# Chunk output matrices before most input matrices, and input matrices that stay on the chip

## Chip, cores, metric

The kernel runs on one core of a Trainium2 chip. The metric is the device time of one execution in microseconds; a comparison goes by the median of several executions.

## The reference, cut to what matters

A two-layer backbone over 1024 latent tokens of 1024 channels and 256 context tokens. The first layer holds 48 groups of a bidirectional linear recurrence (S5) beside an FNet part; the second is pooling and short convolutions. The change lies in the recurrence of the first layer:

```python
def s5_direction(u, lam_re, lam_im, log_step, b_re, b_im, c_re, c_im):
    lam = lax.complex(lam_re, lam_im)
    step = jnp.exp(log_step)[:, None]
    lam_bar = jnp.exp(lam * step)
    b_bar = ((lam_bar - 1.0) / lam)[..., None] * lax.complex(b_re, b_im)
    bu = lax.complex(jnp.einsum('btgh,gph->btgp', u, b_bar.real),
                     jnp.einsum('btgh,gph->btgp', u, b_bar.imag))
    a = jnp.broadcast_to(lam_bar, bu.shape)
    _, s = lax.associative_scan(_linear_recurrence, (a, bu), axis=1)
    return (jnp.einsum('btgp,ghp->btgh', s.real, c_re) - jnp.einsum('btgp,ghp->btgh', s.imag, c_im))
```

It is run over context and latents together, once forward and once backward; u is the first 768 columns of the layer's input projection.

## The kernel before

Channels lie on the 128 partitions. Products are made in three matmuls of split operands (a high part and a low remainder), so each weight tile is first split by `w_split`: ScalarE (ACT) writes the high part, VectorE (DVE) or GpSimd (POOL) subtracts for the low part. TensorE (PE) executes in the order in which the program emits; so does every other engine, and every DMA queue (SP's, POOL's). The program's order is written out by hand: `proj` calls a hook after each of its 8 contraction steps k, and the hook emits other work there.

The recurrence is taken in chunks of 8 steps. For each of 6 blocks b and two halves hf, that is 4 groups at a time:
- a `bl_task` builds an input matrix: five DVE operations write `bl` (with `blp` as scratch), then eight PE transposes and two ACT copies make `bltw`, which POOL's queue stores in DRAM (`bltd`);
- a `cl_task` builds an output matrix: five DVE operations write `cl` (two buffers), two DMAs on SP's queue store it (`cld`), and 32 small matmuls `pz`, ACT copies and two short DVE operations (`dg`, `z`) make the direct term `z`, stored in `zd`;
- `bl_mm(i)` multiplies input matrix i (`blt`, loaded from `bltd`) with the chunked inputs (`ub`, loaded from `ud`) in 32 matmuls, and ACT copies the result into `va` (i under 6) or `vb`.

The order: prelude; then for m = 0 to 5 the projection of 128 columns, 32 per block, to `ut` and its context part `uc` to `utc`, both stored in `ud` by POOL's queue (m = 0 and 1 were multiplied in the prelude). From m = 1 on `fill` is called by the hooks and after each context part: it emits the DVE part of the next task (all 12 bl, then all 12 cl) and, two tasks behind it, that task's PE part. Loads of `blt` and `ub` start in m = 4. Then `fx(0, hook0)` is a projection whose hook emits chunks 0 to 5 and the remaining cl tasks; chunks 6 to 11 follow with `tree(0, l)`, a five-level combination of the context part on `va` (DVE), then `tree(1)` on `vb`, and 121 double scan steps on DVE beside `fx(1)` and eight more projections on PE. Then the outputs are formed (y stage), and the rest of both layers follows.

Two shared sets of buffers matter. `slot` gives one of 8 buffers of 4 KB a partition (tag "slot"); a new tile takes the one given back longest ago, and its first writer waits for the last reader of the old tile. It holds `ut`, `utc`, `bltw`, `blt`, `ub`, `fx`, `zt`. In PSUM there are 4 banks with the tag "m" (`uc`, `pt`, `pz`, a part of the chunk products `vps`) and 4 with "acc" (projections, the rest of `vps`). `raw`, the unsplit weights, has 4 buffers, filled from SP's queue.

Of the kernel before, what the change touches and what calls it, by code (L numbers as in the profile page):

```python
# [194 lines left out]
class Builder:  # L195
# [218 lines left out]
    def s5_prelim(self, tp, s5s, raw):  # L414
# [57 lines left out]
        self.bbs = self.gp.tile([P, NG, 16], F32, name="bbs")  # L472

        def inputs():

            nc.vector.memset(self.bb[:, :, NG], 0.0)
# [12 lines left out]
        self.pwb = self.gp.tile([P, 3, NG, 8], F32, name="pwb")  # L489
        self.pwc = self.kp.tile([P, 3, 9, NG], F32, name="pwc")  # L490
# [15 lines left out]
    def bl_task(self, b, hf):  # L506
# [15 lines left out]
        def pe():  # L522
            blt = self.slot("bltw").rearrange("p (r g n) -> p r g n", r=2, g=4)
            for ri in range(2):
                pt = self.ps("m", "pt")
                for g in range(4):
                    nc.tensor.transpose(pt[:, g * P:g * P + P], bl[:, ri, g].rearrange("p h s -> p (h s)"),  # L527
                                        self.c("ident"))
                self.act(blt[:, ri].rearrange("p g n -> p (g n)"), pt)
            nc.gpsimd.dma_start(self.bltd[b][:, :, 4 * hf:4 * hf + 4], blt)  # L530
        return dve, pe

    def cl_task(self, b, hf):
# [6 lines left out]
        def dve():  # L540
# [165 lines left out]
    def build(self):  # L706
        nc, tc, A = self.nc, self.tc, self.A
        with ExitStack() as es:
# [13 lines left out]
            self.bltd = [self.drp.tile([P, 2, 8, P], F32, name=f"bltd{b}") for b in range(6)]  # L722
# [25 lines left out]
    def layer0(self, es):  # L748
# [5 lines left out]
        self.kp = kx.enter_context(tc.tile_pool(name="kp", bufs=1, side="right"))  # L754
        pwx = ExitStack()
# [183 lines left out]
        tables(0)  # L939
        inputs = inputs()  # L940
        for _ in range(4):
            next(inputs)


        ax = ExitStack()
# [12 lines left out]
        self.sq = nc.sync  # L958
# [19 lines left out]
        blq = []  # L978

        def bl_load(i):  # L980
            b, hf = divmod(i, 2)
            blt = self.slot("blt").rearrange("p (r g n) -> p r g n", r=2, g=4)
            nc.sync.dma_start(blt, self.bltd[b][:, :, 4 * hf:4 * hf + 4])
            ub = self.slot("ub")[:, 0:768].rearrange("p (g j) -> p g j", g=4)
            nc.sync.dma_start(ub, self.ud[b][4 * hf:4 * hf + 4].rearrange("g h s j -> (h s) g j"))
            blq.append((blt, ub))

        for m in range(6):
            if m == 5:
                bl_load(2)  # L990
# [5 lines left out]
            else:  # L996
                self.w_split(names[m + 1])
                self.proj((hi, lo), hr, 8, lambda p, c0, c1: self.act(ut[:, c0:c1], p),
                          hook=(lambda k: fill() if k in ((2, 4, 6, 7) if m == 2 else (0, 2, 4, 6)) else None))
            if m == 1:  # L1000
                tables(1)
                sx.close()
                self.gt = ax.enter_context(tc.tile_pool(name="gt", bufs=1))
                self.kt = kx.enter_context(tc.tile_pool(name="kt", bufs=1, side="right"))
# [21 lines left out]
        ax.close()  # L1026
# [5 lines left out]
        v = [vx.enter_context(tc.tile_pool(name="va", bufs=1)).tile([P, NSTEP, 2, NH], F32, name="va")]  # L1032

        def bl_mm(i):
            blt, ub = blq.pop(0)
# [13 lines left out]
            if i + 3 < 12:  # L1049
                bl_load(i + 3)  # L1050

        blk = list(range(12))
        self.sq = nc.gpsimd

        def fx(ct, hook):
            x = self.slot("fx")
# [3 lines left out]
            self.proj(hl, hr, 8, lambda p, c0, c1: self.act(x[:, c0:c1], p), hook=hook)  # L1060
            return lambda: nc.gpsimd.dma_start(xd[:, ct], x)
# [7 lines left out]
        while pend:  # L1069
            fill()  # L1070
        flush()
        kx.close()
        v.append(vx.enter_context(tc.tile_pool(name="vb", bufs=1, reuse_waits="tile")).tile([P, NSTEP, 2, NH], F32, name="vb"))

        scx = ExitStack()
        scp = scx.enter_context(tc.tile_pool(name="scp", bufs=1, reuse_waits="tile"))
        cf = [self.acf] + [scp.tile([P, 2, 2, NG], F32, name=f"acf{l}") for l in range(1, 5)]

        def square(l):
            r, i = cf[l - 1][:, 0, 0], cf[l - 1][:, 1, 0]  # L1080
            o = cf[l]
            self.mul(o[:, 0, 0], r, r)
            self.mul(o[:, 0, 1], i, i)
            self.stt(o[:, 1, 0], r, 2.0, i, ALU.mult, ALU.mult)
            self.sub(o[:, 0, 0], o[:, 0, 0], o[:, 0, 1])
            self.stt(o[:, 1, 1], r, -2.0, i, ALU.mult, ALU.mult)
# [735 lines left out]
```

## Time and profile before

| | us |
|---|---|
| median of 3 executions | 923.29 (922.24 to 925.9) |
| the profiled execution's own time | 923.49 |
| its span, first to last instruction | 921.7 |
| PE busy in the span | 866.0 (94%) |
| DVE busy | 671.9 (73%) |
| ACT busy | 344.1 (37%) |

The profile is of one execution. Its trace gives start and duration of each instruction, the idle time ahead of it and what ended that (`<-`), and for DMAs when they were issued and when they landed. Matmuls are pipelined, so the duration of one is longer than its share of the time; the distance of starts is what counts. Line 218 is the helper of DVE's additions, subtractions and products, 243 that of ACT's copies, 373 the split matmuls of all projections.

### The profile page before, as it was taken

Reading aid. Unit: us, or ns where it says so; the run is one execution under the profiler, and the core shown is the slowest. Engines: PE = TensorE matmul, PEld = TensorE weight load, DVE = VectorE, ACT = ScalarE, POOL = GpSimd, SP = SyncE. Lnnn points to the kernel's source line nnn. Section 1 sums busy time; section 2 is a strip of 40 time slices with the busy share of each in tenths; the row PEclk is TensorE's granted clock in tenths of the full one; section 3 lists DMA queues with packets and bytes.
Section 4 is the critical chain, followed back from the end, with each engine's and each line's share of the span. In section 5 each row is a group of like instructions: output and inputs, shape, how many; then the busy total and the mean of one; then the engine's idle time right before and its main releaser. Section 6 shows DMA issues by size and latency. Waiting matters only on the chain.

```text
span 921.7 us, 14134 instructions
## 1 busy us (share of the span) xinstructions
PE 866.0 (94%) x5312; PEld 707.6 (77%) x5312; DVE 671.9 (73%) x1736; ACT 344.1 (37%) x593; POOL 94.1 (10%) x91
## 2 busy tenths in 40 slices
PE   9998997989999959899999999999999999989996
PEld 4666785768777738787888999877778778768995
DVE  7787996868999996556367376788885766775354
ACT  5547331465113129644342144542222233453111
POOL 0002330212122203200034001000000000000000
PEclk9999998999999988899999999999999999999998
DMA  9743779891555557931264212121111121261022
GB/s 353 293 137 115 241 215 281 237 368 62 172 217 207 194 172 211 307 127 54 69 250 135 102 41 69 46 58 46 46 47 46 46 65 51 69 228 45 1 92 92
DMA packets 62212, 129.16 MB, mean 140 GB/s; under 512 B 5760, under 2 KB 32560, under 8 KB 62016
## 3 DMA queue, kind: packets, MB, share of 16 engines
q1 hardware_dynamic: 55280, 104.45, 34.2%
q0 software_dynamic: 6864, 23.81, 8.3%
q8 instruction: 42, 0.69, 0.3%
q14 instruction: 26, 0.21, 0.1%
HBM read 100.03 MB, written 28.21 MB: 139 GB/s over the span
## 4 chain that ended last, share of the span: by engine, by line
PE 58%; DVE 26%; ACT 7%; DMA 5%; issue 2%; SPq 1%; ACTq 0%; DVEq 0%; POOL 0%
PE acc L373 32%; PE acc L1743 14%; DVE va L218 11%; DVE vb L218 2%; DVE wlo L218 2%; PE yps L1205 2%; PE acc L883 2%; ACT vb L243 1%; DMA mt<-zd 1%; DVE hh L218 1%; ACT whi L243 1%; DVE tl L218 1%; PE pt L527 1%; DVE xt L218 1%; DMA blt<-bltd 1%
## 5 line engine op out<-in xcount | busy, mean ns | idle before, releaser
L373 PE MATMUL acc<-hh,whi 128*128 128x512 f32 (+1 forms) x352 | 112.1, 385 | 2.5 <-ACT whi L243 2.5
L373 PE MATMUL acc<-hl,whi 128*128 128x512 f32 (+1 forms) x352 | 108.8, 376 | 0.0
L373 PE MATMUL acc<-hh,wlo 128*128 128x512 f32 (+1 forms) x352 | 108.6, 375 | 0.1
L373 PEld LDWEIGHTS acc<-hh,whi 128*128 128x128 f32 x352 | 62.9, 189 | 17.6 <-issue 5.0
L373 PEld LDWEIGHTS acc<-hh,wlo 128*128 128x128 f32 x352 | 65.4, 189 | 13.4 <-DVE wlo L218 0.5
L373 PEld LDWEIGHTS acc<-hl,whi 128*128 128x128 f32 x352 | 65.4, 189 | 13.1
L243 ACT ACTIVATE whi<-hh 128x512 fp32r<-128x512 f32 (+4 forms) x44 | 27.7, 632 | 114.6 <-DVE hh L218 86.0
L218 DVE TENSOR_TENSOR wlo<-raw,whi 128x512 fp32r<-128x512 f32 (+3 forms) x57 | 48.5, 855 | 28.7 <-ACT whi L243 28.2
L243 ACT ACTIVATE whi<-raw 128x512 fp32r<-128x512 f32 (+3 forms) x65 | 51.8, 801 | 42.7 <-PE acc L1743 20.8
L1743 PE MATMUL acc<-th,whi 128*128 128x512 f32 x160 | 63.1, 394 | 0.0
L1743 PE MATMUL acc<-tl,whi 128*128 128x512 f32 x160 | 62.4, 390 | 0.3 <-DVE tl L218 0.3
L218 DVE TENSOR_TENSOR va<-va 128x48 f32<-128x48 f32 (+1 forms) x258 | 62.3, 243 | 0.4
L1743 PE MATMUL acc<-th,wlo 128*128 128x512 f32 x160 | 62.3, 390 | 0.0
L239 DVE SCALAR_TENSOR_TENSOR xl<-acc,adac,xl 128x256 f32<-128x256 f32 (+1 forms) x48 | 27.3, 569 | 41.5 <-PE acc L373 41.1
L218 DVE TENSOR_TENSOR wlo<-hh,whi 128x512 fp32r<-128x512 f32 (+4 forms) x44 | 30.4, 690 | 31.7 <-ACT whi L243 30.9
L1743 PE MATMUL acc<-hh,whi 128*128 128x512 f32 x120 | 48.4, 403 | 5.2 <-DVE y L218 2.5
L1743 PE MATMUL acc<-hh,wlo 128*128 128x512 f32 x120 | 47.5, 396 | 0.3 <-DVE wlo L218 0.3
L1743 PE MATMUL acc<-hl,whi 128*128 128x512 f32 x120 | 47.5, 396 | 0.0
L373 PE MATMUL acc<-hh,wh 128*128 128x256 f32 (+1 forms) x144 | 46.2, 321 | 0.0
L373 PE MATMUL acc<-th,hh 128*128 128x256 f32 (+1 forms) x144 | 46.2, 321 | 0.0
L373 PE MATMUL acc<-hh,wl 128*128 128x256 f32 (+1 forms) x144 | 46.1, 320 | 0.0
L373 PE MATMUL acc<-hl,wh 128*128 128x256 f32 (+1 forms) x144 | 45.9, 318 | 0.0
(295 smaller groups left out, 2125.5 us busy)
## 6 DMA issues: line engine op xcount, KB each, us to landing
raw<-in_ada SPq DMA_DIRECT2D x44, 512.0 KB, 5.7
raw<-in_win SPq DMA_DIRECT2D x38, 512.0 KB, 3.6
raw<-in_wout SPq DMA_DIRECT2D x16, 512.0 KB, 3.7
bltd<-bltw POOLq DMA_DIRECT2D x12, 512.0 KB, 4.9
blt<-bltd SPq DMA_DIRECT2D x12, 512.0 KB, 8.5
cl<-cld POOLq DMA_DIRECT2D x12, 512.0 KB, 6.4
cld<-cl SPq DMA_DIRECT2D x18, 256.0 KB, 5.1
ub<-ud SPq DMA_DIRECT2D x12, 384.0 KB, 7.6
```

The lines of the kernel that those rows point to most:

```text
L218: (eng or self.nc.vector).tensor_tensor(out, a, b, op=op)
L239: self.nc.vector.scalar_tensor_tensor(out, a, s, b, op0=op0, op1=op1)
L243: self.nc.scalar.activation(out, a, func, **kw)
L373: self.nc.tensor.matmul(p, a[:, w], b[:, c0:c1], start=(j == 0 and i == 0), stop=(last and i == 2))
L527: nc.tensor.transpose(pt[:, g * P:g * P + P], bl[:, ri, g].rearrange("p h s -> p (h s)"), self.c("ident"))
L883: nc.tensor.matmul(acc[m][h], a[:, w], b[:, 512 * h:512 * h + 512], start=(k == 0 and i == 0), stop=(k == 7 and i == 2))
L1205: nc.tensor.matmul(ps[:, o], sy[:, ri, g], cl[:, ri, g], start=False, stop=(ri == 1))
L1743: nc.tensor.matmul(ps, x[:, sl], y, start=bool(new and k == 0 and i == 0), stop=(k == 3 and i == 2), skip_group_check=True)
```

## The change

Input matrices are no longer stored in DRAM and loaded: ACT copies the transposes into a slot (`blt`) from which `bl_mm` reads. `bl` becomes a slot, `blp` a PSUM tile of tag "m", `bbs` a slot. The order of tasks becomes: bl 0 to 2, all 12 cl, bl 3 and 4 in m = 1 to 5 (17 calls of `fill`); then `chunk(i)` emits, for i over 2, the transposes of matrix i, the product, and the DVE part of matrix i + 2, so that bl 5 to 11 are built between the chunks. Chunks 0 to 9 now lie in the hooks of `fx(0)`: two after k = 0, two after k = 1, one after each other k; `square` and `tree(0)` follow chunk 5 in the hook of k = 3 and take three slots; chunks 10 and 11 follow, with the split of weight 8 and six scan steps of `va` between them. `ub` is loaded two chunks ahead, from after the loop on. `cld` and `zd` are stored by POOL's queue. `tables(0)` (ACT's six `pwb` copies) moves from the end of the prelude to m = 0, behind the split of weight 2. Slots for `fx` and `zt` are taken when they are first written. `va` and `vb` are opened together.

```diff
@@ bl_task
-        bl = self.gt.tile([P, 2, 4, 16, 8], F32, tag="bl", name="bl", bufs=2)
+        bl = self.slot("bl").rearrange("p (r g h s) -> p r g h s", r=2, g=4, h=16)
-            p = self.gt.tile([P, 4, 16, 8], F32, tag="blp", name="blp", bufs=1)
+            p = self.ps("m", "blp").rearrange("p (g h s) -> p g h s", g=4, h=16)
-            blt = self.slot("bltw").rearrange("p (r g n) -> p r g n", r=2, g=4)
+            blt = self.slot("blt").rearrange("p (r g n) -> p r g n", r=2, g=4)
...
-            nc.gpsimd.dma_start(self.bltd[b][:, :, 4 * hf:4 * hf + 4], blt)
+            self.blts.append(blt)
@@ cl_task
-                self.sq.dma_start(self.cld[b][r, :, 4 * hf:4 * hf + 4], cl[r, :, :, o:o + 128])
+                nc.gpsimd.dma_start(self.cld[b][r, :, 4 * hf:4 * hf + 4], cl[r, :, :, o:o + 128])
@@ layer0
-        tables(0)
         inputs = inputs()
-        for _ in range(4):
+        for _ in range(2):
             next(inputs)
...
-        todo = []
-        for b in range(6):
-            todo += [(self.bl_task, b, 0), (self.bl_task, b, 1)]
-        for b in range(6):
-            todo += [(self.cl_task, b, 0), (self.cl_task, b, 1)]
+        bls = [(self.bl_task, b, hf) for b in range(6) for hf in range(2)]
+        todo = bls[:3] + [(self.cl_task, b, hf) for b in range(6) for hf in range(2)] + bls[3:5]
+        bls = bls[5:]
...
-                self.sq.dma_start(self.zd[b].rearrange("a p e -> p a e"), z)
+                nc.gpsimd.dma_start(self.zd[b].rearrange("a p e -> p a e"), z)
...
-            if len(pend) == 2 or not todo:
-                if pend:
-                    pend.pop(0)()
+            if len(pend) == 2:
+                pend.pop(0)()
...
-            if m == 4:
-                bl_load(0)
-                bl_load(1)
...
             if m == 0:
                 self.w_split(names[2])
+                tables(0)
                 for _ in inputs:
                     pass
-            else:
+            elif m < 3:
                 fill()
...
+        while todo:
+            fill()
+        flush()
+        kqx.close()
...
+        ub_load(0)
+        ub_load(1)
 
         def bl_mm(i):
-            blt, ub = blq.pop(0)
+            blt, ub = self.blts.pop(0), ubq.pop(0)
...
-            if i + 3 < 12:
-                bl_load(i + 3)
+            ub_load(i + 2)
+
+        def chunk(i):
+
+            if i > 2:
+                pend.pop(0)()
+            bl_mm(i)
+            if i > 2 and bls:
+                f, b, hf = bls.pop(0)
+                t = f(b, hf)
+                t[0]()
+                pend.append(t[1])
...
+        def square():
+
+            t = self.slot("acf")[:, 0:16 * NG].rearrange("p (l k r g) -> p l k r g", l=4, k=2, r=2)
...
+        def tree(c):
+
+            tr = [self.slot("tr") for k in range(2)]
+            for l in range(5):
...
         def hook0(k):
-            if k not in (2, 5):
-                bl_mm(blk.pop(0))
-                fill()
+            for i in {0: (0, 1), 1: (2, 3)}.get(k, (k + 2,)):
+                chunk(i)
+            if k == 3:
+                square()
+                tree(0)
...
-        while blk:
-            bl_mm(blk.pop(0))
-            if len(blk) == 0:
-                self.w_split(names[8], nc.gpsimd)
-            if len(blk) < 5:
-                tree(0, 4 - len(blk))
+        chunk(10)
+        self.w_split(names[8], nc.gpsimd)
         for i in range(NC_, NC_ + SKEW):
             step((0, i))()
-        for l in range(5):
-            tree(1, l)
+        chunk(11)
+        kx.close()
+        tree(1)
```

## Rows read from the trace of the kernel before

**Rows 1.** Stretches: us, busy of PE, PEld, DVE, ACT, POOL, PEclk, DMA share, GB/s.

```profile
81.85:162.30 80.45, 74.05 (x553) 58.57 (x554) 69.94 (x112) 29.21 (x64) 20.47 (x27) 0.96 0.82 247
162.30:214.70 52.40, 47.72 (x650) 39.72 (x648) 37.59 (x105) 31.98 (x65) 9.79 (x13) 1.00 0.88 278
330.60:341.70 11.10, 2.21 (x34) 1.09 (x28) 11.10 (x83) 1.20 (x3) 0.71 (x1) 0.78 0.35 94
```

**Rows 2.** Chain of waits, 60 to 230 us: start, us, what.

```profile
193.22 8.78 DMA blt<-bltd
```

**Rows 3.** Timeline around the start of m=2: start, us, engine, line, operation [idle <-releaser].

```profile
74.01 5.60 ACT L243 ACTIVATE pwb<-pw 64x384 f32<-64x384 f32 x6
80.74 1.06 ACT L243 ACTIVATE whi<-raw 128x1024 fp32r<-128x1024 f32 x1
81.85 0.73 PE L373 MATMUL acc<-hh,whi 128*128 128x512 f32 x2 [2.47 <-ACT whi L243]
```

**Rows 4.** DVE's timeline in m=2 to 5, and a group from the groups by line.

```profile
94.32 0.69 DVE L218 TENSOR_TENSOR blp<-bbs,pwb 128x512 f32<-128x512 f32 x1
...
97.46 0.69 DVE L218 TENSOR_TENSOR blp<-bbs,pwb 128x512 f32<-128x512 f32 x1
...
140.93 0.23 DVE L239 SCALAR_TENSOR_TENSOR dg<-cst,vec,pz 128x16 f32<-128x16 f32 x1
...
144.62 1.22 DVE L218 TENSOR_TENSOR wlo<-raw,whi 128x1024 fp32r<-128x1024 f32 x1
...
L218 DVE TENSOR_TENSOR hl<-acc,hl 128x512 f32<-128x512 f32 x20 | 13.7, 683 | 0.0
```

**Rows 5.** Chain of waits, PE's pieces in m=2 to 5.

```profile
107.27 0.87 PE pt L527 x8
108.15 2.80 PE acc L373 x12
116.90 2.87 PE uc L373 x24
133.11 0.64 PE pz L566 x32
```

**Rows 6.** Instructions by tile: bltw; then landings of tiles ut, ub and cl.

```profile
L243 ACT ACTIVATE bltw<-pt x24: 592/598/603, 90.4 to 130.4; 128x512 f32<-128x512 f32 x24
L530 POOL DMA_DIRECT2D bltd<-bltw x12: 667/676/1156, 91.8 to 131.3; - x12
...
DMA to landing us min/median/max: 4.0/5.0/6.2
...
DMA to landing us min/median/max: 4.9/7.6/13.6
...
DMA to landing us min/median/max: 3.4/6.5/8.9
```

**Rows 7.** PE's timeline, first matmuls of two neighbouring chunks.

```profile
209.86 0.32 PE L1042 MATMUL vps<-ub,blt 128*64 128x160 f32 x1
...
212.27 0.32 PE L1042 MATMUL vps<-ub,blt 128*64 128x160 f32 x1
```

**Rows 8.** DVE's timeline: squares, tree(0), first scan step.

```profile
194.87 0.32 DVE L218 TENSOR_TENSOR acf<-acf 128x48 f32<-128x48 f32 x2
...
198.84 1.82 DVE L218 TENSOR_TENSOR tr<-va,acf 128x768 f32<-128x768 f32 x2 [1.11 <-ACT va L243]
200.59 1.94 DVE L218 TENSOR_TENSOR va<-va,tr 128x768 f32<-128x768 f32 x2
...
207.66 0.26 DVE L218 TENSOR_TENSOR va<-va,acf 128x96 f32<-128x96 f32 x1
```

**Rows 9.** Stretch after a wait of PE; columns as in rows 1.

```profile
157.67:162.73 5.06, 5.03 (x41) 3.62 (x42) 3.00 (x7) 1.54 (x6) 0.00 (x0) 0.50 1.02 286
```

**Rows 10.** Timelines of DVE and POOL at tree(1).

```profile
217.55 4.14 DVE L218 TENSOR_TENSOR vb<-vb,tr 128x768 f32<-128x768 f32 x2
...
216.72 3.17 POOL L218 TENSOR_TENSOR wlo<-raw,whi 128x1024 fp32r<-128x1024 f32 x1 [16.15 <-ACT whi L243]
```

More of the change, by code (lines that the diff above doesn't have):

```diff
@@ L471, in s5_prelim @@
         self.bb = self.kp.tile([P, 2, NG + 1, 16], F32, name="bb")
[L472 removed]
         def inputs():
+            self.bbs = self.slot("bbs")[:, 0:NG * 16].rearrange("p (g h) -> p g h", g=NG)
             nc.vector.memset(self.bb[:, :, NG], 0.0)
@@ L486, in inputs @@
                 yield
-        self.pwb = self.gp.tile([P, 3, NG, 8], F32, name="pwb")
-        self.pwc = self.kp.tile([P, 3, 9, NG], F32, name="pwc")
+        self.pwb = self.kp.tile([P, 3, NG, 8], F32, name="pwb")
+        self.pwc = self.kq.tile([P, 3, 9, NG], F32, name="pwc")
         self.acf = self.pwp.tile([P, 2, 2, NG], F32, name="acf")
@@ L998, in layer0 @@
                 self.proj((hi, lo), hr, 8, lambda p, c0, c1: self.act(ut[:, c0:c1], p),
-                          hook=(lambda k: fill() if k in ((2, 4, 6, 7) if m == 2 else (0, 2, 4, 6)) else None))
+                          hook=lambda k: fill() if k in ((2, 4, 6) if m == 2 else (0, 2, 4, 6)) else None)
             if m == 1:
@@ L1048, in bl_mm @@
                     self.act(dst, src)
-            if i + 3 < 12:
-                bl_load(i + 3)
-        blk = list(range(12))
-        self.sq = nc.gpsimd
+            ub_load(i + 2)
[8 more added lines that the diff above has]
+                pend.append(t[1])
+        cf = [self.acf]
+        def square():
+            t = self.slot("acf")[:, 0:16 * NG].rearrange("p (l k r g) -> p l k r g", l=4, k=2, r=2)
+            cf.extend(t[:, l] for l in range(4))
+            for l in range(1, 5):
+                r, i = cf[l - 1][:, 0, 0], cf[l - 1][:, 1, 0]
+                o = cf[l]
+                self.mul(o[:, 0, 0], r, r)
+                self.mul(o[:, 0, 1], i, i)
+                self.stt(o[:, 1, 0], r, 2.0, i, ALU.mult, ALU.mult)
+                self.sub(o[:, 0, 0], o[:, 0, 0], o[:, 0, 1])
+                self.stt(o[:, 1, 1], r, -2.0, i, ALU.mult, ALU.mult)
+                nc.vector.tensor_copy(o[:, 0, 1], o[:, 0, 0])
+        def tree(c):
+            tr = [self.slot("tr") for k in range(2)]
+            for l in range(5):
+                n = NC_ >> (l + 1)
+                d = 1 << l
+                a, b = (v[c][:, k * d - 1:NC_:2 * d] for k in (1, 2))
+                gs = slice(NH * c, NH * c + NH)
+                tm = [t[:, 0:2 * NH * n].rearrange("p (n r g) -> p n r g", n=n, r=2) for t in tr]
+                for k in range(2):
+                    self.mul(tm[k], a, cf[l][:, k, :, gs].unsqueeze(1).to_broadcast([P, n, 2, NH]))
+                self.add(b, b, tm[0])
+                self.add(b, b, tm[1][:, :, ::-1])
         def fx(ct, hook):
-            x = self.slot("fx")
             hl = self.w_take(names[6 + ct])
@@ L1059, in fx, with evac @@
                 self.w_split(names[7])
-            self.proj(hl, hr, 8, lambda p, c0, c1: self.act(x[:, c0:c1], p), hook=hook)
-            return lambda: nc.gpsimd.dma_start(xd[:, ct], x)
-        def hook0(k):
-            if k not in (2, 5):
-                bl_mm(blk.pop(0))
-                fill()
-        fx(0, hook0)()
[L1069 to L1086, printed above, removed]
-            nc.vector.tensor_copy(o[:, 0, 1], o[:, 0, 0])
-        def tree(c, l):
-            n = NC_ >> (l + 1)
-            d = 1 << l
-            a, b = (v[c][:, k * d - 1:NC_:2 * d] for k in (1, 2))
-            gs = slice(NH * c, NH * c + NH)
-            tm = [scp.tile([P, NC_ // 2, 2, NH], F32, tag=f"tr{k}", name="tr", bufs=1)[:, 0:n] for k in range(2)]
-            for k in range(2):
-                self.mul(tm[k], a, cf[l][:, k, :, gs].unsqueeze(1).to_broadcast([P, n, 2, NH]))
-            self.add(b, b, tm[0])
-            self.add(b, b, tm[1][:, :, ::-1])
+            x = []
+            def evac(p, c0, c1):
+                if not x:
+                    x.append(self.slot("fx"))
+                self.act(x[0][:, c0:c1], p)
+            self.proj(hl, hr, 8, evac, hook=hook)
+            return lambda: nc.gpsimd.dma_start(xd[:, ct], x[0])
+        def hook0(k):
+            for i in {0: (0, 1), 1: (2, 3)}.get(k, (k + 2,)):
[3 more added lines that the diff above has]
+                tree(0)
+        fx(0, hook0)()
         def step(*ci):
@@ L1117, in step @@
             return f
-        for l in range(1, 5):
-            square(l)
-        while blk:
-            bl_mm(blk.pop(0))
-            if len(blk) == 0:
-                self.w_split(names[8], nc.gpsimd)
-            if len(blk) < 5:
-                tree(0, 4 - len(blk))
+        chunk(10)
+        self.w_split(names[8], nc.gpsimd)
         for i in range(NC_, NC_ + SKEW):
             step((0, i))()
-        for l in range(5):
-            tree(1, l)
+        chunk(11)
+        kx.close()
+        tree(1)
         n = NSTEP - 1
@@ L1136, in layer0 @@
         store = fx(1, lambda k: self.bg(2 if k % 4 else 1))
-        zt = [self.slot(f"zt{k}") for k in range(KD)]
+        zt = []
         gates = [(0, ch) for ch in range(8, 12)] + [(1, ch) for ch in range(12)]
```

37 lines of the change are left out of this document (18 added, 19 removed).

## The prediction

> **What bounds the kernel now.** I read the table of stretches first. It shows TensorE (PE) busy nearly everywhere, so a gain must come from its gaps and from places where VectorE (DVE) sets the end. Two stretches belong to the change: 81.85 to 162.3 us (input projections m=2 to 5, with 12 input-matrix and 6 output-matrix tasks between them; PE idles 6.4 us) and 162.3 to 214.7 us (the fx projection with the 12 chunk inputs; 4.7 us). Then DVE runs tree(1) and the scan steps without a break, and PE has run out of work at 330.6 to 341.7, where it is busy 2.2 of 11.1 us while DVE is busy all of it [rows 1]. So what follows the last chunk hangs on DVE, and an earlier last chunk moves the end one for one. I therefore follow three times: when m=2 starts, t0 = the end of projection m=5 (162.3), and the end of the last chunk (214.7). The chain of waits names the DMA round trip of the input matrices in the second stretch: reading one back took 8.8 us [rows 2].
>
> **The head.** Today ScalarE (ACT) makes the six `pwb` copies (5.60 us) ahead of `ut` and of the split of weight 2, and PE waits 2.47 us for that split [rows 3]. The change moves `tables(0)` behind the split. The split then ends at about 76.2, its low half on DVE at 77.6, and PE starts m=2 at 79.4. The copies now precede `utc`, the second `ut` and `pwc`, so the split of weight 3 still ends near 88.6: DVE waits about 3 us for it after the first input-matrix task, and the second task ends at 92.9. PE meets its transposes at 89.8 and stalls 3.1 us; a few waits of under 1 us bring this to 4.4.
>
> **m=2 to 5.** A bl task takes DVE 3.13 us, a cl task with its `dg` 3.69, a low half 1.14 (from 94.32 to 97.46, from 140.93 to 144.62, and its row of 1.22 less the overlap with the next) [rows 4]. `blp` in PSUM I take at no cost: a same-sized DVE add with a PSUM operand took 683 ns, as the SBUF ones do [rows 4]; the bounds are 0 and some 0.1 us for each of 3 operations in 12 tasks, hidden where DVE waits. On PE one k of a projection takes 1.40, a context part 2.87, a set of transposes 0.87, a `pz` 0.7 (0.64 in its row, and a little to start) [rows 5]. From 79.4 to t0: 32 k at 1.40 (44.9) + 3 context parts (8.6) + 3 transposes (2.6) + 12 pz (8.4) = 64.5, + 4.4 idle = 68.9, so 148.3. DVE needs in the same time bl0 to bl2, twelve cl and four low halves, and reaches cl11 at 144, just ahead of PE's last hook. They are balanced, and the cover is thin.
>
> The `cld` stores go from SP to POOL's queue. Two cl buffers mean that cl task i+2 writes only when store i has landed. POOL issued the 512 KB stores in 0.68 us each; `cld` stores landed 3.4 to 8.9 us after issue, median 6.5 [rows 6]. With two issues of 0.75 and a landing in light traffic I take 5.5 us from the end of the task to the landing; two tasks then need 2.67 + 5.5 = 8.2 us, against PE's 8.5 (17.05 for each m with 4 tasks). So little is lost; 0 to 6 us, I take 1.2, nearer the free end because 12 stores and all read-backs of the input matrices leave. POOL's in-order queue also puts `ud` stores behind `cld` stores, which nobody awaits before m=5. t0 = 149.5, which is 12.8 earlier.
>
> The 12 stores and 12 loads of input matrices that go free 12 issues of POOL and 12 of SP (0.68 us and more each); no engine waits for these issues, so that is worth nothing but quieter DMA. The `zd` stores move to POOL as well; their buffers come round only every fourth task, so I put them at nothing, covered by two tasks of 3.69.
>
> A rule bears on this move. In this trace POOL's issue took 0.68 us while DVE computed almost without pause [rows 4, 6]. The Trainium skill (SBUF — State Buffer, section SBUF: two separate sides) says that GpSimd writes the descriptors of such DMAs and is locked out while DVE runs an operation in a two-port mode. If these DVE operations were of that kind, each of a task's two issues would wait for up to one of them, and the sum would be that of the slower rival below; the trace disagrees for these operations.
>
> **After t0.** PE's own work is a context part 2.9 + fx 11.2 + 12 chunks at 2.41 [rows 7] (28.9) + 9 transposes that moved here (7.8) = 50.8, against 52.4 measured with all its idle time [rows 1]. So nothing is gained here, and three things are added.
>
> First, the loads of `ub`. Until now they start during m=4. In the change `ub_load(0)` and `(1)` stand behind the loop, and of the eight slots six hold `bbs`, blt0 to 2, bl3 and bl4; the other two are `ut` and `utc` of m=5. So ub0 waits until `ut` is stored: ACT ends about 1 us after t0, the store lands 4.0 to 6.2 us after issue, and a `ub` load takes at least 4.9 [rows 6]: about t0 + 10. PE arrives at t0 + 4.4 and waits 5.6. ub1 waits for the two `utc` stores and lands near t0 + 14.6, after chunk 0 (t0 + 12.4): 2.2 more. Later loads start two chunks ahead and are hidden by these. 7.8 us; bounds 5 and 12.
>
> Second, `square` and `tree(0)` take three slots (`acf`, two `tr`) behind chunk 5. Live then are `bbs`, bl6, bl7, ub6, ub7: all eight are gone. So blt6 gets a `tr` buffer, ACT waits at its copy until tree(0) ends, and PE waits for blt6 at chunk 6. tree(0) ran from 198.84 to 207.66, 8.8 us, with squares of 2.9 us before it [rows 8]; in the old order both ran beside chunks. From the end of chunk 5: ACT's last copy 0.8 (or bl7 and the squares, about 1), tree 8.8, copy and start 0.8, less 2.3 of PE work there is (one k and the transposes): 8.5 us; bounds 7.5 and 10.5. Queued behind: on ACT nothing else, on DVE nothing that PE needs.
>
> Third, transposes now stand directly before the chunk that reads them. ACT's copy takes 0.60 each [rows 6], so PE waits 0.3 to 0.9, I take 0.5, nine times: 4.5.
>
> Both long waits pull the clock down: after the wait that ended at 157.67 the next 5.06 us ran at 0.50 of full speed, 1.2 instead of 2.4 GHz [rows 9], worth about 2 us by the doubled matmul times, twice: 4. Chunk phase: 50.8 + 7.8 + 8.5 + 4.5 + 4 = 75.6, against 52.4: +23.2.
>
> **The tail.** tree(1) holds a pair of adds that took 4.14 us, where the same pair of tree(0) took 1.94 [rows 8, 10]: POOL's low half of weight 8 ran from 216.72 to 219.89. The change splits weight 8 before chunk 11, so that this falls into the first scan steps, which finish before the chunk does: -2.2. The steps themselves do not change, and slots for `fx` and `zt` that are taken only at their first write wait for nothing that the old order did not.
>
> **Sum.** -12.8 + 23.2 - 2.2 = +8.2 us on the profiled execution's 923.5, which is 0.2 above the median: 931.7.
>
> **Rivals.**
> Faster: the new waits do not bind, because the loads or slots come free as early as today. Then the phase is 50.8 + 4.5 + 1 = 56.3, +3.9, and the sum -11.1: 912. For it speaks that 12.8 us before t0 rest on counted work; against it the count of eight slots. Between this and the forecast the change breaks even: when the 24.8 us of stalls after t0 shrink below 16.6. That middle ends at 919 to 928.
> Slower still: the landing of `cld` from POOL's queue becomes the pace of m=2 to 5. With 7.0 us from task to landing two tasks need 9.7, 0.6 a task over PE's pace, 7 us in all: 938. The long landings before (8.9) came while the input matrices were read back, which is against it. The rule named above leads here.
> The change does not do what it says: tiles of ACT and DVE order otherwise than I read, so t0 moves little. With t0 only 8 earlier: 936.
>
> **Chances.** Forecast and its own range of 924 to 937: 0.58; slower rivals 0.14; middle 0.16; faster 0.12. Range 919 to 941: it leaves out the faster rival and the far ends. 0.5% (4.6 us) is about what a measurement can tell from no change: faster 0.12, same 0.22 (the middle and the forecast's low edge), slower 0.66.
>
> **What would show it.** PE's m=2 starting near 79.4 without the 2.47 us wait; t0 near 149.5; PE idle before the first chunk matmul, ended by the `ub` load, 5 to 6 us; idle at chunk 6 that ends with a copy released by tree(0), 8 us, with a granted clock of 0.50 behind each; no 4 us pair in tree(1); DVE's end of steps as far behind the last chunk as now, less 2.2. I am wrong if t0 comes much earlier or later, or if PE runs through chunk 6.

## The result, and the profile after

The changed kernel takes 933.41 us (median of 4 executions, 931.64 to 936.35), the kernel before 922.76 in the same comparison (921.68 to 925.9): a ratio of 1.0113, 95% interval 1.0077 to 1.0149. It is slower by 10.7 us. The prediction was 931.7, +8.2 us.

The profiled execution of the changed kernel has a span of 934.6 us, against 921.7. The first view is the table of stretches, with the columns of [rows 1]: from the first matmul of m=2 to the first of m=5's context part (t0), and from t0 to the end of the last chunk.

```profile
80.65:162.97 82.32, 72.49 (x675) 55.56 (x673) 66.17 (x113) 26.09 (x63) 33.89 (x43) 0.94 0.70 178
162.97:231.47 68.50, 56.70 (x530) 48.68 (x528) 41.63 (x106) 41.58 (x72) 6.25 (x6) 0.92 0.35 101
```

The kernel before, cut at the same two matmuls, for comparison:

```profile
81.85:162.13 80.28, 73.88 (x552) 58.40 (x553) 69.78 (x112) 29.04 (x64) 20.47 (x27) 0.96 0.82 247
162.13:214.66 52.53, 47.85 (x650) 39.84 (x648) 37.76 (x105) 32.12 (x65) 9.79 (x13) 0.99 0.88 278
```

m=2 to 5 did not get shorter, though nine sets of transposes left it and only six of pz came; the chunk phase grew by 16.0. PE is idle 9.83 us in the first (82.32 less 72.49) and 11.80 in the second. The granted clock in this trace is 1.0 or 0.5 (2.4 or 1.2 GHz), so means of 0.94 and 0.92 stand for some 10 us at the lower level in each stretch.

PE's timeline with its idle times in brackets, a few rows of each part:

```profile
80.65 0.62 PE L373 MATMUL acc<-hh,whi 128*128 128x512 f32 x2
...
95.22 1.94 PE L527 MATMUL pt<-cst,bl 128*128 128x128 f32 x8 [3.74 <-DVE bl L218]
...
117.31 0.41 PE L566 MATMUL pz<-cl,bb 64*32 64x128 f32 x4 [2.10 <-DVE cl L218]
...
159.42 0.90 PE L566 MATMUL pz<-cl,bb 64*32 64x128 f32 x30 [2.40 <-ACT z L243]
...
171.61 0.50 PE L1036 MATMUL vps<-ub,blt 128*64 128x160 f32 x1 [4.10 <-DMA ub<-ud]
...
199.96 0.35 PE L1036 MATMUL vps<-ub,blt 128*64 128x160 f32 x1 [0.69 <-ACT blt L243]
207.28 0.35 PE L1036 MATMUL vps<-ub,blt 128*64 128x160 f32 x1 [2.46 <-ACT blt L243]
...
224.24 0.35 PE L1036 MATMUL vps<-ub,blt 128*64 128x160 f32 x1 [1.52 <-ACT blt L243]
229.08 0.35 PE L1036 MATMUL vps<-ub,blt 128*64 128x160 f32 x1 [1.42 <-ACT blt L243]
...
358.90 1.22 PE L1210 MATMUL yps<-cl,sy 128*128 128x128 f32 x4 [9.28 <-ACT sy L243]
```

The 2.47 us wait of [rows 3] is gone; the idle times of the chunk phase are the first ub load (4.10), the tree (2.46) and ACT's copies (eight of 0.25 to 1.52, 5.25 together), which add up to the 11.80.

Why ACT's z came so late at 159.42 is told by ACT's timeline and by POOL's queue ahead of it:

```profile
138.51 0.76 ACT L243 ACTIVATE z<-pz 128x128 f32<-128x128 f32 x4 [7.64 <-DMA zd<-z]
...
159.09 0.43 ACT L243 ACTIVATE z<-pz 128x128 f32<-128x128 f32 x2 [10.32 <-DMA zd<-z]
```

```profile
149.22 0.90 POOL L1009 DMA_DIRECT2D ud<-ut  x1
150.02 0.97 POOL L1012 DMA_DIRECT2D ud<-utc  x1
150.81 1.06 POOL L1013 DMA_DIRECT2D ud<-utc  x1
151.57 0.99 POOL L957 DMA_DIRECT2D zd<-z  x1
152.56 1.53 POOL L556 DMA_DIRECT2D cld<-cl  x2
```

Six stores in a row. The view of DMAs gives, for the stretch 149 to 153.9, the share of the 16 DMA engines that POOL's queue (q0) and SP's (q1) took, and KB and median us from issue to landing; then the landings for 143.9 to 148.6, where cld stores stand on the queue alone:

```profile
q0 software_dynamic: 199, 0.68, 56.9%
q1 hardware_dynamic: 144, 0.52, 41.5%
...
cld<-cl POOLq DMA_DIRECT2D x3, 256.0 KB, 7.4
ud<-ut POOLq DMA_DIRECT2D x1, 512.0 KB, 6.9
ud<-utc POOLq DMA_DIRECT2D x2, 128.0 KB, 6.9
zd<-z POOLq DMA_DIRECT2D x1, 240.0 KB, 7.4
```

```profile
cld<-cl POOLq DMA_DIRECT2D x4, 256.0 KB, 3.8
```

The same store lands in 3.8 us alone and in 7.4 around the three ud stores. A cld store directly ahead of these is late as well: the one issued at 107.5, followed at 108.25 by three ud stores, landed 7.4 us after its issue, and DVE waited for its buffer:

```profile
115.07 1.43 DVE L218 TENSOR_TENSOR cl<-cb,pwc 128x576 f32<-128x576 f32 x2 [2.73 <-DMA cld<-cl]
```

Of the 6.6 us that DVE waits for cld stores in all, 4.9 end with such a store from ahead of the ud stores and 1.6 with one from behind. In the first stretch SP's queue moves a weight load at the same time, and the two queues together keep the engines 98% busy. So place in the queue and traffic are not parted by these rows.

Over the whole execution the page gives these medians, which answer to [rows 6]:

```profile
cld<-cl POOLq DMA_DIRECT2D x24, 256.0 KB, 4.8
...
ub<-ud SPq DMA_DIRECT2D x12, 384.0 KB, 3.4
```

At tree(1) DVE's pair of adds now takes 1.94 us in place of the 4.14 of [rows 10]:

```profile
234.35 1.94 DVE L218 TENSOR_TENSOR vb<-vb,tr 128x768 f32<-128x768 f32 x2
```

And PE's wait ahead of the outputs, 9.28 us above, was this in the kernel before:

```profile
343.90 1.22 PE L1205 MATMUL yps<-cl,sy 128*128 128x128 f32 x4 [11.09 <-ACT sy L243]
```

Last, a difference ahead of the change. The same instructions of the prelude ran 2.77 us later in this execution, because of a stretch at half clock that the profiled execution of before has not:

```profile
26.70:33.52 6.82, 6.82 (x40) 6.12 (x43) 3.50 (x11) 2.12 (x8) 0.00 (x0) 0.50 1.03 413
```

The kernel before had one of 3.41 us at 73.99, in the context parts of m=0 and 1. So times are compared below as lengths of stretches, not by the clock on the wall.

| stretch, us | before | predicted | after |
|---|---|---|---|
| first matmul of m=0's context part to that of m=2 | 12.14 | 9.7 | 8.17 |
| m=2 to t0 | 80.28 | 70.1 | 82.32 |
| t0 to the end of the last chunk | 52.53 | 75.6 | 68.50 |
| last chunk to the first matmul on sy | 129.24 | 127.0 | 127.43 |

The number came out near, the way to it did not: two stretches are off by 12.2 and by -7.1 us, and it was luck that these errors have opposite signs.

### The profile page after: what moved, and what is told of

It is laid out like the page before. It is cut to its first block, busy times and chain, and to the rows that moved or that the text cites. A ratio compares the mean times of both kernels' runs of the same rounds, so it can differ in the third digit from the quotient of the medians.

```text
span 934.6 us, 14093 instructions
## 1 busy us (share of the span) xinstructions
PE 873.2 (93%) x5312; PEld 712.5 (76%) x5312; DVE 670.6 (72%) x1736; ACT 345.8 (37%) x593; POOL 101.4 (11%) x100
## 4 chain that ended last, share of the span: by engine, by line
PE 53%; DVE 23%; ACT 5%; DMA 5%; issue 3%; POOL 1%; DVEq 0%; ACTq 0%; SPq 0%; POOLq 0%
PE acc L373 30%; PE acc L1748 15%; DVE va L218 11%; DMA cld<-cl 3%; PE vps L1036 3%; DVE vb L218 2%; DVE wlo L218 1%; DMA mt<-zd 1%; DVE tl L218 1%; ACT whi L243 1%; DVE cl L218 1%; PE yps L1210 1%; ACT sy L243 1%; DVE hh L218 1%; DVE bl L218 1%
```

## Experiments: the stores of m=2 to 5

Theory: the stores on POOL's queue make m=2 to 5 wait, for buffers of z and cl. First a third z buffer:

```diff
-self.z = self.kt.tile([P, 2, 240], F32, tag="z", name="z", bufs=2)
+self.z = self.kt.tile([P, 2, 240], F32, tag="z", name="z", bufs=3)
```

> The changed kernel with three z buffers in place of two, nothing else. In the changed kernel's trace ScalarE (ACT) waits 7.64 and 10.32 us for a zd store to land, and TensorE (PE) then idles 2.40 us at 159.42. Theory (the store of z, queued on POOL behind three ud stores, holds ACT, DVE and PE): both waits of ACT go, PE's 2.40 us goes, and with it most of a 3.4 us stretch at half clock: the end of projection m=5 comes 2.5 to 4.5 us earlier and the time falls from 933.4 to 929 to 931. Rival (the wait is replaced by the next one, the landing of cld on two cl buffers, which DVE meets anyway): PE idles as long in m=5, ended by DVE cl, and the time moves by less than 1 us.

934.49 us, ratio 1.0116 (1.0092 to 1.014), the same as the change. In the profiled execution m=2 to 5 takes 77.79 us and ACT's waits for zd are gone, but DVE's waits for cld landings grew from 6.6 to 8.4 us, and PE still idles 7.24 us. The time shows nothing of it. So the rival holds for the time; in the trace it holds in part, since DVE's waits took the place of ACT's, but PE idles only 1.4 us in m=5 in place of 3.7.

Then four cl buffers beside the three of z:

```diff
-cl = self.kt.tile([P, 2, 4, 144], F32, tag="cl", name="cl", bufs=2)
+cl = self.kt.tile([P, 2, 4, 144], F32, tag="cl", name="cl", bufs=4)
```

> The changed kernel with three z and four cl buffers, so that no output-matrix task waits for a store. Theory (the landings of cld and zd stores cost PE the idle 2.27 us in m=3 and 3.8 us in m=5, and the half clock behind each): DVE's waits for cld (6.6 us in five) and for z (5.0 us in two) go, PE idles under 1 us in m=3 to 5, the end of projection m=5 comes 6 to 9.5 us earlier, and the time is 924 to 927.5. Rival (DVE's own work is the bound of m=3 to 5, 66 us busy of 82): PE's idle time stays above 4 us, ended by DVE cl without a wait of DVE, and the time falls by 2 us at most.

925.59 us, ratio 1.0023 (1.0008 to 1.0039): 0.9%, some 8 us, come back. The table of stretches of this run:

```profile
78.56:150.22 71.66, 67.94 (x675) 52.71 (x673) 66.31 (x115) 26.15 (x62) 33.83 (x43) 0.98 0.76 200
150.22:220.02 69.80, 56.64 (x530) 48.58 (x528) 40.93 (x103) 41.77 (x72) 6.24 (x6) 0.93 0.35 103
```

m=2 to 5 is 10.7 us shorter, and of PE's 3.72 us of idle time all is the wait of the head (3.72 <- DVE bl). DVE is as busy as before (66.31 us against 66.17); its own work was not the bound. Four cl buffers without the third z were not tried.

And the stores on SP's queue, with two buffers each:

```diff
-nc.gpsimd.dma_start(self.cld[b][r, :, 4 * hf:4 * hf + 4], cl[r, :, :, o:o + 128])
+nc.sync.dma_start(self.cld[b][r, :, 4 * hf:4 * hf + 4], cl[r, :, :, o:o + 128])
...
-nc.gpsimd.dma_start(self.zd[b].rearrange("a p e -> p a e"), z)
+nc.sync.dma_start(self.zd[b].rearrange("a p e -> p a e"), z)
```

> The changed kernel with its cld and zd stores back on SP's queue, as in the kernel before; two buffers each, as there. Theory (both things count: the zd store is late because it queues behind ud stores on POOL, but the cl waits come from two buffers and landings of 3.4 to 8.3 us, which SP's queue does not shorten): the waits for zd go, the waits for cld stay near 6 us; end of projection m=5 2.5 to 4.5 us earlier, time 929 to 931. Rival one (POOL's queue is the whole cause, for cld too): cld lands in under 5 us throughout and the gain is that of four buffers, 6 to 9.5 us, 924 to 927.5. Rival two (on SP the stores stand behind weight loads that wait for a buffer): waits grow and the time is above 934.

927.71 us, ratio 1.0039 (1.002 to 1.0058): between the theory and rival one.

```profile
78.88:154.35 75.47, 69.48 (x674) 53.75 (x672) 66.13 (x113) 27.25 (x64) 12.01 (x14) 0.95 0.75 191
```

m=2 to 5 is 6.8 us shorter than with POOL's queue, 3.8 longer than with more buffers. So of the 10.7 us some two thirds go with the queue, and the rest stays with two buffers on SP's queue too. The waits got shorter, they did not go: ACT waits 13.1 us for zd (18.0 in the changed kernel), DVE 4.2 us for cld (6.6); the longest landing of a zd store is 5.6 us (7.6), of a cld store 6.9 (8.3). I had put the cld waits down to the buffers alone; that was wrong.

## Experiments: single waits of the chunk phase

One scratch slot in the trees, so that a slot more is free:

```diff
-tr = [self.slot("tr") for k in range(2)]
+tr = self.slot("tr")
...
-    self.mul(tm[k], a, ...)
-self.add(b, b, tm[0])
-self.add(b, b, tm[1][:, :, ::-1])
+    self.mul(tm, a, ...)
+    self.add(b, b, tm if k == 0 else tm[:, :, ::-1])
```

> The changed kernel with tree(0) and tree(1) working in one scratch slot, their two products one after the other, so that one slot more stays free; same operations on DVE. Theory (chunk 7's blt takes a slot that tree(0) still uses; PE idles 2.46 us at 207.28 and runs 3.4 us at half clock behind it): the wait goes, the last chunk ends 2.5 to 4 us earlier, time 929.5 to 931. Prediction's size (8.5 us for this stall and some 2 for the clock): 923 to 925. Rival (DVE's next input-matrix tasks stand behind the tree anyway, so PE waits for bl one or two chunks later): idle moves to chunk 8 or 9, time within 1 us of 933.4.

933.23 us, ratio 1.0103 (1.0083 to 1.0123): no difference that shows. The 2.46 us are gone from chunk 7, and at the next transposes there is

```profile
208.59 1.60 PE L527 MATMUL pt<-cst,bl 128*128 128x128 f32 x8 [1.84 <-DVE bl L218]
```

The rival: the tasks queued on DVE behind the tree are late as well.

The first two ub loads early, in slots that bl3 and bl4 leave free, since these two are now made behind the loop:

```diff
-        todo = bls[:3] + [(self.cl_task, b, hf) for b in range(6) for hf in range(2)] + bls[3:5]
-        bls = bls[5:]
+        todo = bls[:3] + [(self.cl_task, b, hf) for b in range(6) for hf in range(2)]
+        bls = bls[3:]
...
+            if m == 5:
+                ub_load(0)
+                ub_load(1)
...
+        todo, bls = bls[:2], bls[2:]
         while todo:
             fill()
...
-        ub_load(0)
-        ub_load(1)
```

> The changed kernel with the first two ub loads issued at the start of m=5 and the input-matrix tasks bl3 and bl4 made after the loop in place of inside m=5, which frees the two slots for the loads. Theory (the first chunk waits only for slots and the load): PE's 4.10 us wait before the first chunk goes and with it the 6.83 us at half clock that cover chunks 0 to 2; the last chunk ends 5 to 7.5 us earlier, time 926 to 928.5. Rival (the wait moves to the transposes of bl3 or bl4, which DVE makes later): PE idles 3 us or more at chunk 3 or 4, ended by DVE bl, and the time is within 2 us of 933.4. By the prediction's own terms (7.8 us for the loads and some 2 for the clock) 923.5.

933.39 us, ratio 1.0117 (1.0093 to 1.0142). The wait came back in another form:

```profile
167.00 0.53 PE L1038 MATMUL vps<-ub,blt 128*64 128x160 f32 x1 [4.79 <-DVE bl L218]
...
176.22 0.32 PE L1038 MATMUL vps<-ub,blt 128*64 128x160 f32 x1 [3.42 <-DMA ub<-ud]
```

A chunk's matmul reads no bl; what it waits for is the PSUM bank of `blp`. DVE had written `blp` and then stood 6.23 us for a slot (ended by a ud store) before it could write bl, and held the bank all that time. So a shortage of slots reaches PE through PSUM.

Transposes right behind the chunk before:

```diff
-            if i > 2:
-                pend.pop(0)()
             bl_mm(i)
...
+            if i > 1 and pend:
+                pend.pop(0)()
```

> The changed kernel with each chunk's transposes right behind the chunk before it, so that a k of the fx projection lies between them and their reader; nothing else. Theory (PE waits for ACT's copy of each blt: .50, .25, .25, .69, 2.46, .31, .31, 1.52 and 1.42 us in the changed kernel's trace, 7.7 in all): the waits of chunks 3 to 10 fall to under 0.2 us each, that of tree(0) goes to another place or goes, PE idles 3 to 5 us less in the chunk phase, time 928.5 to 930.5. The prediction's 0.5 each, nine times, says 4.5: 929. Rival (DVE's bl is then what PE waits for, since transposes come earlier and the tasks do not): PE idle ended by DVE bl instead, time within 1.5 us of 933.4.

932.98 us, ratio 1.0101 (1.0076 to 1.0126). The time goes to the rival. The copies' waits fall as expected, but that of the tree doubles, since a transpose now comes sooner and the tree does not:

```profile
205.50 0.53 PE L1036 MATMUL vps<-ub,blt 128*64 128x160 f32 x1 [5.19 <-ACT blt L243]
```

All of these edits at once, with the four cl and three z buffers:

> The changed kernel with three z and four cl buffers, one scratch slot in the trees, early ub loads and transposes one chunk ahead. Theory (the stores on two buffers cost m=2 to 5 some 10 us; the first ub wait, the copies and the clock behind them cost the chunk phase 8 to 12): from the 925.6 of the run with more buffers another 8 to 12 us go, 914 to 918, under the kernel before (ratio 0.990 to 0.996). Rival (in the chunk phase DVE, with five squares, a tree and nine input-matrix tasks, is the bound, so that waits only change their names): chunk phase still over 65 us, 922 to 926, no better than the kernel before.

931.85 us, ratio 1.0092 (1.0056 to 1.0127), 6 us worse than the buffers alone. m=2 to 5 takes 70.9 us, the chunk phase 76.5, with 20 us of idle time:

```profile
164.74 0.53 PE L1038 MATMUL vps<-ub,blt 128*64 128x160 f32 x1 [7.68 <-DVE bl L218]
...
206.96 1.97 PE L527 MATMUL pt<-cst,bl 128*128 128x128 f32 x8 [6.70 <-DVE bl L218]
```

The earlier t0 comes, the slot wait of DVE becomes 14.80 us, and PE meets it through PSUM. That is the rival's side and worse than it said: the waits were not just renamed, they grew. A further 3.81 us of PE, at 169.35, end with ACT's copy to va, and ACT had stood 13.33 us until 168.30, put down to the last zd store. That is another wait than the one for slots; the runs on the first chunk below take it apart.

## Experiment: head and tail alone

The kernel before with `tables(0)` behind the split of weight 2, and the split of weight 8 ahead of the last two chunks:

```diff
-        tables(0)
...
                 self.w_split(names[2])
+                tables(0)
...
+            if len(blk) == 2:
+                self.w_split(names[8], nc.gpsimd)
             bl_mm(blk.pop(0))
-            if len(blk) == 0:
-                self.w_split(names[8], nc.gpsimd)
```

> The kernel before with the two steps of the change that need no new buffers: tables(0) and the rest of bb made behind the split of weight 2, and the split of weight 8 issued ahead of the last two chunks' work (POOL's low half in place before tree(1)). The input matrices still go through DRAM, all tasks in the old order. Theory (both ends are real terms): PE's 2.47 us wait at the start of m=2 goes and 1 to 2.5 us of it are left at t0; tree(1) loses its 4.14 us pair, the wait before the outputs shrinks from 11.1 to about 9; time 3 to 4.5 us below the kernel before, ratio 0.995 to 0.997. Rival (m=2 to 5 of the kernel before are bound by DVE, busy 70 of 80 us, and give the head back): t0 within 0.5 us of before relative to the start of m=0, time only some 2 us lower, ratio 0.998.

922.9 us, ratio 0.9996 (0.9979 to 1.0013). The first row below is its stretch of m=2 to 5, the second the wait ahead of the outputs:

```profile
78.72:163.45 84.73, 74.75 (x554) 60.77 (x553) 69.94 (x113) 33.15 (x69) 20.33 (x26) 0.93 0.75 231
```

```profile
343.41 1.22 PE L1205 MATMUL yps<-cl,sy 128*128 128x128 f32 x4 [10.05 <-ACT sy L243]
```

m=2 starts 8.17 us after m=0's context part, as in the change, and m=2 to 5 is 4.5 us longer: PE's idle time goes from 6.40 to 9.98, and the clock falls more. The head is given back in full. Of the tail about 1 us is left (11.09 to 10.05), though DVE's pair of adds takes 1.95 us here too. The expected 3 to 4.5 us did not come; the rival holds.

## Experiments: the first chunk, and the order behind it

From here on with four cl and three z buffers. ut and utc of m=5 in tiles of their own, so that two slots are free for ub in m=5:

```diff
-            ut = self.slot("ut")
+            ut = self.slot("ut") if m < 5 else self.kt.tile([P, T], F32, name="ut5")
+            if m == 5:
+                ub_load(0)
+                ub_load(1)
...
-            uc = self.slot("utc")[:, 0:TC].rearrange("p (s j) -> p s j", s=8)
+            uc = (self.slot("utc") if m < 5 else self.kt.tile([P, TC], F32, name="utc5"))[:, 0:TC]
+            uc = uc.rearrange("p (s j) -> p s j", s=8)
...
-        ub_load(0)
-        ub_load(1)
```

> The run with three z and four cl buffers, and ut and utc of m=5 in tiles of their own, so that two slots are free at the start of m=5, where the first two ub loads are now issued; the input-matrix tasks stay where the change has them. Theory (the first chunk waits for slots alone, and in the run with early loads the wait came back only because bl3 and bl4 then stood in the same queue for slots): PE's wait before the first chunk (5.50 us in the run with more buffers) goes, with most of the 6.83 us at half clock behind it; chunk phase 61 to 64 in place of 69.8, time 918 to 921. Rival (va lies where the closed pool was, so that the first copies of ACT wait for the ud stores of m=5, which land some 9 us after t0): PE idles 3 us or more inside chunk 0 or 1, ended by ACT va, time 923 to 926.

926.09 us, ratio 1.0041 (1.0021 to 1.0061): no gain, the rival's sign. PE's idle row, ACT's and POOL's:

```profile
164.33 0.53 PE L1038 MATMUL vps<-ub,blt 128*64 128x160 f32 x1 [5.31 <-ACT va L243]
```

```profile
163.31 2.33 ACT L243 ACTIVATE va<-vps 128x480 f32<-128x480 f32 x4 [6.63 <-DMA ub<-ud]
```

```profile
157.57 0.88 POOL L957 DMA_DIRECT2D zd<-z  x1
```

That store of the last z, behind the three ud stores of m=5, landed 5.6 us after its issue, and ACT starts with that, at 163.31. With more cl buffers the closed pool reaches under va, and z lies there; the releaser that the profile names (a ub load) is not the one; in the next run the same wait is put down to zd<-z. In the changed kernel itself z lies under vb, so this second guard is one that the larger pool brought.

On top of it the tree's one scratch slot as above, and squares and bl5 in another place:

```diff
-            if i > 2 and bls:
+            if i == 0:
+                square()
+            if i in (1, 3, 4, 6, 7, 8, 9) and bls:
...
             if k == 3:
-                square()
                 tree(0)
```

> The run before it, and then: the squares made right behind chunk 0, where DVE has nothing to do; the tree with one scratch slot; the input-matrix task of bl5 made behind chunk 1 and none behind chunk 5, the others behind chunks 3, 4 and 6 to 9. Same operations on every engine. Theory (from chunk 3 on DVE is the bound: seven input-matrix tasks of 3.13 us, squares of 3.8 and a tree of 8.7 make 34.4 us, which DVE starts only at chunk 3 and then works off almost without a break, so that taking single waits of PE away moved nothing): PE idles under 4 us from chunk 3 on, chunk phase 57 to 60, time 914 to 917. Rival (PE's work and its waits for ACT's copies set the pace, DVE has slack): chunk phase within 1.5 us of the run before it.

928.14 us, ratio 1.0061 (1.0037 to 1.0085). The wait for the last zd is there again (5.82 us of PE), now under its name:

```profile
164.12 2.32 ACT L243 ACTIVATE va<-vps 128x480 f32<-128x480 f32 x4 [7.15 <-DMA zd<-z]
```

Behind chunk 3 nearly every chunk still waits 0.31 to 2.25 us, for ACT's copies and once for DVE. The chunk phase takes 69.3 us against 68.0 in the run before it; the rival holds, and DVE's work alone is not the bound.

All zd stores off POOL's queue, and ub loaded behind bl3 and bl4; the rest as in the run with free slots:

```diff
-nc.gpsimd.dma_start(self.zd[b].rearrange("a p e -> p a e"), z)
+nc.sync.dma_start(self.zd[b].rearrange("a p e -> p a e"), z)
...
-            if m == 5:
-                ub_load(0)
-                ub_load(1)
...
+                          (ub_load(0), ub_load(1)) if (m, k) == (5, 7) else None)
```

> The run with free slots for the first ub loads, with two edits: the zd stores go from SP's queue, and the two ub loads are issued at the end of projection m=5, behind bl3 and bl4, which so get the slots that are free early. In the run before, ACT's first copy of a chunk waited until 163.31, 11 us after t0, for the store of the last z, which stands on POOL behind three ud stores and in whose memory va lies. Theory (two waits of about the same date guard the first chunk, the slots of ub and the memory under va, so that taking one away moved nothing): with both gone PE idles under 1.5 us between t0 and the end of chunk 1 and the half clock there goes, chunk phase 60 to 63 in place of 68 to 70, time 917 to 920. Rival (a third store under va or vb, of cld or ud, lands as late): PE idles over 3 us there, ended by ACT va, 923 to 926.

920.81 us, ratio 0.9971 (0.9957 to 0.9986). The chunk phase is 63.6 us, its mean granted clock 0.97, and the longest wait at its start 1.27 us (table of stretches, then PE's timeline):

```profile
151.84:215.46 63.62, 54.26 (x530) 45.94 (x528) 40.94 (x103) 41.41 (x72) 5.49 (x5) 0.97 0.38 115
```

```profile
159.86 0.35 PE L1036 MATMUL vps<-ub,blt 128*64 128x160 f32 x1 [1.27 <-ACT va L243]
```

That is just above what was expected (63 and 920). So with the larger pool the first chunk had two guards, two things to wait for that end at about the same time: the slots of the first loads and the store under va. Taking away the first alone moved nothing, both together some 5 us; the second alone was not tried.

And the order of the chunk phase, with one scratch slot:

```diff
-            if i > 2:
-                pend.pop(0)()
             bl_mm(i)
+            if i > 1 and pend:
+                pend.pop(0)()
+            if i == 0:
+                square()
-            if i > 2 and bls:
+            if i in (1, 2, 3, 4, 6, 7, 8):
                 f, b, hf = bls.pop(0)
...
```

> The same with the chunk phase rearranged, no operation added or left out: squares behind chunk 0, one scratch slot for the tree, transposes right behind the chunk before, bl5 to bl8 made behind chunks 1 to 4, the tree behind chunk 5, bl9 to bl11 behind chunks 6 to 8. Theory (what is left of the chunk phase's waits, 8 us in nine waits for ACT's copies and the tree, is order: DVE idles 16 us before chunk 3 and is then a task behind): PE idles under 4 us in the whole phase, chunk phase 55 to 58, near the 52.5 of the kernel before, and the time is 912 to 916. Rival (slots: eight do not hold a task more ahead, so that the same idle time comes back under other names): chunk phase within 2 us of the run beside it.

913.51 us, ratio 0.9894 (0.9881 to 0.9908), under both kernels: some 10 us less than the kernel before, some 20 less than the change as it was made. The chunk phase in the table of stretches, and its two longest waits behind chunk 3:

```profile
150.63:206.78 56.15, 52.10 (x530) 43.90 (x528) 41.87 (x103) 39.65 (x72) 4.07 (x5) 1.00 0.43 130
```

```profile
199.38 0.66 PE L527 MATMUL pt<-cst,bl 128*128 128x128 f32 x4 [0.72 <-DVE bl L218]
...
204.39 0.35 PE L1036 MATMUL vps<-ub,blt 128*64 128x160 f32 x1 [1.00 <-ACT blt L243]
```

PE works 52.1 us of 56.2 at full clock, and no wait of over 1 us for the tree is left: bl5 to bl8 are built ahead of it (bl5 to bl7 in the change). The theory holds, time and stretch as expected. Which of the edits against the run before carries the 7 us was not tried one by one.

## Why the prediction was right, and where it was not

**Head.** Right: no 2.47 us wait, m=2 8.17 us after m=0's context part against some 9.7 (79.4 less 69.7), the rest being the half clock that before had there. The stall at the second transposes was 3.74 against 3.1.

**m=2 to 5.** The step that failed is the cover of the stores. cld stood in the sum at 1.2 us with bounds of 0 and 6, zd at nothing; with buffers enough the stretch is 71.66, so both cost 10.7 with the clock. The price of 5.5 us holds two issues of 0.75, so some 4 us for a landing; that was near the median (4.8 on the page after) and too low around the ud stores, where cld stores landed after 5.8 to 8.3 us. I noted that POOL's queue puts ud stores behind cld ones, and didn't turn it round: three ud stores stand ahead of the next cld, twice ahead of the next zd too (issued at 130.82 and 151.57), and the cld directly ahead of them is late as well. The cover of zd, two tasks of 3.69, fell with it, since ACT waits up to 10.32 us. The kernel before could have shown this: with the same two buffers, on SP's queue, DVE and ACT stood in m=5 for

```profile
155.52 1.43 DVE L218 TENSOR_TENSOR cl<-cb,pwc 128x576 f32<-128x576 f32 x2 [4.54 <-DMA cld<-cl]
```

```profile
159.84 0.76 ACT L243 ACTIVATE z<-pz 128x128 f32<-128x128 f32 x4 [13.81 <-DMA zd<-z]
```

so neither store was covered there, and the change takes twelve such tasks in this stretch in place of six. (The 3.4 to 8.9 us of [rows 6] include the loads of the output stage that read cld back; the stores alone took 3.4 to 8.3, and six of the 24 already stood on POOL's queue.) The same sum without these stores was good (its 17.05 for an m is 16.9 by its own terms, which changes nothing): 70.1, less the 1.2 for cld, against 71.66. Of that rest 1.7 is a half clock of 3.41 us, and a pz costs 0.84 in place of 0.70 (starts 3.64 apart with two k of 1.40 between):

```profile
104.24 0.71 PE L566 MATMUL pz<-cl,bb 64*32 64x128 f32 x32
...
107.88 0.71 PE L566 MATMUL pz<-cl,bb 64*32 64x128 f32 x32
```

The slower rival had this place and its sign, with 7 us. Its other root, the issue on POOL, did not show: a cld issue took 0.75 us all through, at most 0.79, beside a busy DVE, so no issue was held up as the rule in the prediction would have it. The Trainium skill has a second rule that bears on it (DMA: Bandwidth & Descriptors, section Issuing engines are not separate DMA queues): DMAs of all issuing engines run on the same 16 DMA engines, and issuing from several saves only issue time. The trace bears out the first half, as both queues together kept the engines 98% busy around the ud stores. Whether the second half holds here is not shown: the same stores from SP made the stretch 6.8 us shorter, and how much of that is issue time saved (the six issues in a row stand from 149.22 to 154.09 on POOL) and how much the shorter landings, no run parts.

**After t0.** 75.6 against 68.50. PE's work (50.8) and the clock (4, measured 10.5 us at half, so 5) hold, and the copies too (4.5 against 5.25). Two terms were too large. The tree's stall is 2.46, not 8.5 (the terms of that sum add up to between 8.1 and 8.3): the step that failed is the count of slots. blt6 takes the buffer of bl6 itself, whose last readers are the transposes that fill it, so no ninth slot is needed; the first blt to get a `tr` buffer is blt7, and by then a chunk more has run beside the tree. The loads' wait is 4.10, not 7.8: a ub load lands in 3.4 us (median, page after; 7.6 in [rows 6]), so the 4.9 was no lower bound, and chunk 0 at half clock hides ub1. That the loads are faster because the DMA engines are less busy (0.35 of the chunk phase in place of 0.88, by the table of stretches) is likely, but no run shows it by itself.

**Tail.** Right: -2.2 forecast, -1.8 measured at the wait ahead of the outputs (11.09 to 9.28 us), and no 4 us pair.

**The sum.** Head -2.5, m=2 to 5 -10.3, chunk phase +23.2, tail -2.2 were forecast as length changes; measured are -4.0, +2.0, +16.0 and -1.8, and +0.7 in the rest of the two profiled executions (+2.8 ahead of the change, -2.1 behind it). The prediction named two signs of being wrong, and both came: t0 at 162.97 in place of 149.5, and a PE that all but runs through chunk 6 (0.69 us). The wait ahead of the first chunk, 4.10 us, lies under its 5 to 6 as well. So the mechanism failed in two places, and the number came out near by luck, because an error of 12.2 us too little and one of 7.1 too much had opposite signs.

**What stays open.** Whether the third z buffer alone is worth anything (its profiled stretch says 4.5 us, its time nothing), how much of the late landings is order on POOL's queue and how much traffic, and how the last 7 us are split.

## What to carry to other kernels

A store moved to another queue shares it with the bursts that stand there: here it landed late both ahead of them and behind them, so look for the bursts, not for the median, and ask who needs its buffer. Where waits share one resource (slots here), taking them away one at a time showed nothing or made another grow; find all guards of the same date, remove them together, and only then mend the order. Compare the forecast by stretches, since a sum can be right with wrong terms.

## What the runs showed of the hardware that I had not expected

A 256 KB store took 3.4 to 4.1 us alone and 7.1 to 8.3 behind 768 KB on the same queue, with a weight load on the other; issued directly ahead of these 768 KB it took 5.8 to 7.4. The prelude, the same in both kernels, ran 6.82 us at half clock in one profiled execution and not in the other, though PE was busy in all of that stretch and in 6.43 of the 6.70 us ahead of it; such stretches moved single profiles by 1.7 and 2.8 us here, and only lengths of stretches and repeated times can be compared.
